# Two transformer blocks on one core: the four FFN up products in Strassen's form

## The chip, the cores and the metric

The kernel runs on 1 core of a Trainium2 chip. The metric is the time of one execution on the device in microseconds (us): 2631.76 us, the median of 3 runs (2631.64 to 2631.97). The core's engines are TensorE (PE; its weight loads are PEld), VectorE (DVE), ScalarE (ACT), GpSimd (POOL) and SyncE (SP), which issues most DMAs.

## What is computed

512 tokens of 1024 channels pass four layers, each a mixer and an FFN with norms and a residual. The mixers (forgetting attention, a gated recurrence, stick-breaking attention with a pool, gated linear attention) are the same in both kernels. Layers 0 and 1 have the SwiGLU FFN, layers 2 and 3 the convolutional one; 2816 hidden channels, gate and up side by side in one weight matrix of 1024 x 5632.

```python
def swiglu_ffn(h, w_in, w_out):
    gate, up = jnp.split(jnp.einsum('bsd,df->bsf', h, w_in), 2, axis=-1)
    return jnp.einsum('bsf,fd->bsd', jax.nn.silu(gate) * up, w_out)

def conv_ffn(h, w_up, conv_w, conv_b, w_down):
    s = h.shape[1]
    u = h @ w_up
    up = jnp.pad(u, ((0, 0), (CONV_WIDTH - 1, 0), (0, 0)))
    conv = conv_b
    for j in range(CONV_WIDTH):
        conv = conv + conv_w[j] * up[:, j:j + s]
    a, g = jnp.split(conv, 2, axis=-1)
    return (jax.nn.silu(a) * g) @ w_down
```

## The kernel before

Activations lie with channels on partitions, 512 tokens in the columns. Every operand of a large product is held as two parts, hi + lo == x: ScalarE casts x to hi, VectorE subtracts to get lo (`split`, L122 to L130). A product is three passes, hi x hi, hi x lo and lo x hi (`mm3`, L242 to L249), so each line L244, L246, L248 has a third of the matmuls.

Weights stream in chunks of 128x1024 fp32, in the order of the `specs` list (`plan_up`, `plan_out` and others): a DMA on SP's queue into one of three raw buffers, a cast (L158) and a subtraction (L159; on GpSimd for chunks marked `early`) into a slot. The slots are W0 to W2, and R or X tiles while they are free. A slot is free again when its matmuls are done (`release`).

An up stage: `up_first` runs six column tiles of 128 for one half of the tokens (256 columns a matmul), while `norm_chain` makes the norm of the other half; its `spread` (L318) puts a value for each token on all partitions. Then come the other half and the remaining column tiles at 512 columns a matmul, two gate tiles and two up tiles in turn. `swiglu_evac` or `conv_evac` takes each finished pair from PSUM (tiles `g`, `a`), computes silu and the product (for the convolution L634 to L636 on ScalarE and VectorE, the last multiply L644 on GpSimd) and splits the result into `hid` (L126, L127). The down product follows.

TensorE issues in the order of the program (`in_order`); small matmuls of a chain are put between the products by a count of columns (`spawn`, `tick`, `due`). The order on the other engines comes from a scheduler at build time. Each engine works through its list in that order.

## Time and profile before

| what | value |
|---|---|
| median of the runs | 2631.76 us |
| profiled execution, span from first to last instruction | 2630.8 us |
| TensorE busy | 2567.0 us, 98%, 13789 matmuls |
| VectorE busy | 1256.5 us, 48% |
| ScalarE busy | 944.0 us, 36% |
| GpSimd busy | 369.0 us, 14% |
| mean granted TensorE clock | 0.989 |
| DMA | 216.91 MB, mean 82 GB/s |

The span and the median differ by 1.0 us, so durations of the profile can be set against the runs. Busy time of TensorE counts overlapping matmuls once; one matmul of 512 columns is shown as 0.39 us long, though the next starts 0.23 us after it. What a stage costs is therefore read from starts, not from durations. Idle time of the other engines costs nothing as long as TensorE doesn't wait for them.

### The profile page before, as it was taken

The page shows a single profiled execution, that of the slowest core. Times are in us where ns is not written, and L with a number is a line of the kernel's source. Part 1 is how long each engine was busy: PE and PEld are TensorE (multiplying, and loading weights), DVE is VectorE, ACT ScalarE, POOL GpSimd, SP SyncE. Part 2 cuts the span into 40 slices and gives each one's busy share as a digit, 9 for nine tenths or more (in the row PEclk, how much of TensorE's full clock was granted, in tenths as well). Part 3 has the DMA queues.
Part 4 walks back from the last instruction along what each step waited for, and adds up shares of the span by engine and source line. Part 5 has one row for each costly group of instructions (what it writes and reads, how often), then busy time and mean ns, then how long its engine had stood idle before and what let it go on. Part 6 is the DMA issues. An engine that isn't in the chain of part 4 may idle for free.

```text
span 2630.8 us, 34163 instructions
## 1 busy us (share of the span) xinstructions
PE 2567.0 (98%) x13789; PEld 2136.0 (81%) x13789; DVE 1256.5 (48%) x2025; ACT 944.0 (36%) x1604; POOL 369.0 (14%) x362
## 2 busy tenths in 40 slices
PE   8999899999899998999999999999999999999999
PEld 6677888888899988988888768888888668888888
DVE  5666543342455564433324675455523344555531
ACT  4445432232222234322323463344422434344421
POOL 0000310000421113000003323111102001211100
PEclk9999999999899999999999999999999999999999
DMA  4223113232212122123322122122332213233331
GB/s 132 72 71 100 58 57 96 91 122 93 81 46 65 52 97 64 56 90 96 120 96 77 57 73 65 57 93 92 120 96 66 65 56 105 65 96 96 96 124 45
DMA packets 224602, 216.91 MB, mean 82 GB/s; under 512 B 9213, under 2 KB 214619, under 8 KB 224443
## 3 DMA queue, kind: packets, MB, share of 16 engines
q1 hardware_dynamic: 222907, 210.15, 25.6%
q0 software_dynamic: 1456, 4.53, 0.6%
q8 instruction: 109, 1.79, 0.3%
q14 instruction: 50, 0.41, 0.1%
q10 hardware_dynamic: 80, 0.03, 0.0%
HBM read 212.55 MB, written 2.13 MB: 82 GB/s over the span
## 4 chain that ended last, share of the span: by engine, by line
PE 92%; DVE 5%; issue 1%; ACT 1%; POOL 0%; DMA 0%; DVEq 0%; ACTq 0%; POOLq 0%
PE g L246 26%; PE g L248 26%; PE g L244 26%; PE a L244 2%; PE a L246 1%; PE a L248 1%; DVE ar L159 1%; PE a L1082 1%; PE m L1082 1%; PE a L1124 1%; PE m L1523 1%; PE m L244 1%; DVE acc L299 1%; DVE h L337 1%; DVE sums L342 0%
## 5 line engine op out<-in xcount | busy, mean ns | idle before, releaser
L159 DVE TENSOR_TENSOR ar<-raw,ar 128x1024 fp32r<-128x1024 f32 (+1 forms) x308 | 381.4, 1239 | 523.1 <-ACT ar L158 522.3
L248 PE MATMUL g<-X,ar 128*128 128x512 f32 (+1 forms) x1568 | 598.9, 383 | 2.6 <-DVE ar L127 2.6
L246 PE MATMUL g<-X,ar 128*128 128x512 f32 (+1 forms) x1568 | 593.7, 379 | 1.5 <-DVE X L127 1.2
L244 PE MATMUL g<-X,ar 128*128 128x512 f32 (+1 forms) x1568 | 589.4, 377 | 5.0 <-ACT ar L126 2.4
L246 PE MATMUL g<-ar 128*128 128x512 f32 (+1 forms) x1608 | 564.6, 351 | 0.2 <-DVE ar L127 0.2
L244 PE MATMUL g<-ar 128*128 128x512 f32 (+1 forms) x1608 | 552.5, 345 | 3.3 <-ACT ar L126 2.6
L248 PE MATMUL g<-ar 128*128 128x512 f32 (+1 forms) x1608 | 552.7, 344 | 0.0
L158 ACT CAST ar<-raw 128x1024 fp32r<-128x1024 f32 (+1 forms) x342 | 354.3, 1038 | 515.0 <-PE g L246 378.9
L246 PEld LDWEIGHTS g<-X,ar 128*128 128x128 f32 x1568 | 297.6, 190 | 66.1 <-DVE X L127 2.3
L244 PEld LDWEIGHTS g<-X,ar 128*128 128x128 f32 x1568 | 296.7, 190 | 65.9 <-ACT ar L126 3.2
L248 PEld LDWEIGHTS g<-X,ar 128*128 128x128 f32 x1568 | 297.5, 190 | 60.3 <-DVE ar L127 3.7
L244 PEld LDWEIGHTS g<-ar 128*128 128x128 f32 x1608 | 307.1, 191 | 41.5 <-issue 6.5
L246 PEld LDWEIGHTS g<-ar 128*128 128x128 f32 x1608 | 308.6, 192 | 31.4 <-issue 3.9
L248 PEld LDWEIGHTS g<-ar 128*128 128x128 f32 x1608 | 308.6, 192 | 27.2 <-issue 1.7
L644 POOL TENSOR_TENSOR a<-a,sg 128x512 f32<-128x512 f32 x44 | 75.1, 1709 | 417.5 <-ACT a L634 323.5
L299 POOL TENSOR_TENSOR acc<-acc,sq 128x512 f32<-128x512 f32 x19 | 27.8, 1464 | 676.1 <-ACT sq L298 623.1
L159 DVE TENSOR_TENSOR X<-raw,X 128x1024 fp32r<-128x1024 f32 (+1 forms) x52 | 57.1, 1099 | 115.5 <-ACT X L158 115.5
L158 ACT CAST X<-raw 128x1024 fp32r<-128x1024 f32 (+1 forms) x60 | 57.7, 962 | 131.2 <-PE g L246 104.3
L159 POOL TENSOR_TENSOR ar<-raw,ar 128x1024 fp32r<-128x1024 f32 x34 | 83.1, 2445 | 126.4 <-ACT ar L158 126.4
L248 PE MATMUL g<-ar,X 128*128 128x512 f32 (+1 forms) x256 | 90.5, 354 | 0.0
L244 PE MATMUL g<-ar,X 128*128 128x512 f32 (+1 forms) x256 | 90.3, 353 | 0.0
L246 PE MATMUL g<-ar,X 128*128 128x512 f32 (+1 forms) x256 | 90.3, 353 | 0.0
(387 smaller groups left out, 3232.7 us busy)
## 6 DMA issues: line engine op xcount, KB each, us to landing
raw<-in_ffn_w_in_dram SPq DMA_DIRECT2D x88, 512.0 KB, 3.4
raw<-in_ffn_w_up_dram SPq DMA_DIRECT2D x88, 512.0 KB, 3.6
raw<-in_ffn_w_out_dram SPq DMA_DIRECT2D x40, 512.0 KB, 3.3
raw<-in_ffn_w_down_dram SPq DMA_DIRECT2D x40, 512.0 KB, 3.4
...
```

Of the source, the lines that this page charges most:

```text
L158: nc.scalar.copy(hi, raw)
L159: (nc.gpsimd if s.early else nc.vector).tensor_sub(lo, raw, hi.bitcast(F32))
L244: mm(ps, ah, bh, start=start, stop=False)
L246: mm(ps, ah, bl, start=False, stop=False)
L248: mm(ps, al, bh, start=False, stop=stop)
L299: eng.tensor_add(acc[:, cols], acc[:, cols], sq[:, :n])
L337: eng.tensor_add(hv, hv, tmp)
L644: nc.gpsimd.tensor_mul(g, g, us[m])
L1082: mm(ps[:M, tt * 64 : (tt + 1) * 64].rearrange("p (b i) -> p b i", i=H), h["k"][:, tt * P : tt * P + M], qv[:, tt * nb // 4 : (tt + 1) * n ...
L1124: nc.tensor.matmul(po[:, c[tt]], lhs, vb[:, s, w], start=s == 0, stop=s == tt)
L1523: mm(po[i * 64 : i * 64 + 64, h * HS : (h + 1) * HS], q[:, 2 * b + h, ck * 64 : (ck + 1) * 64], state[h], start=True, stop=True)
```

## The change

The up product is written as [X11 X12; X21 X22] times [B11 B12; B21 B22]: the rows of blocks are the two halves of the tokens, the inner blocks the two halves of the 1024 channels, the columns 256 gate and 256 up columns. For each of the 11 column blocks seven products of half the size take the place of eight, by Strassen's algorithm in Winograd's variant. Their left operands are a11, a12, s1, s2, s4, s3, a22, made once for an FFN by `combine` in the norm; their right operands are four weight chunks and three differences and a fourth, b12 - b11, b22 - (b12 - b11), b22 - b12, b21 - (...), made in the raw buffers by `pump` before the split (L192), on the engines that `SW` and `CV` name. The results are added while they leave PSUM. The convolution now reads copies in SBUF (`g`, `u`), since its outputs are sums of several products.

`hid` is held in fp32 between up and down; `down` splits it, tile by tile, at its first use. In the up stage there are four slots (W0 to W3) and six raw buffers. The R region changes sides with every FFN; X slots open after down's first column pair. Comment lines are gone throughout.

```diff
-            if slot is None:
+            if slot is None or any(k not in self.raws for k in s.loads):
                 return
             self.free.discard(slot)
+            if s.prep:
+                out, x, y, eng = s.prep
+                getattr(nc, eng).tensor_sub(self.raws[out][1], self.raws[x][1], self.raws[y][1])
             n = s.nk * s.nc
-            reg, o = self.slot_at[slot]
-            hi, lo = reg[:, o : o + n], reg[:, o + 1024 : o + 1024 + n]
-            raw = self.raws.pop(self.n_split)[:, :n]
+            reg = self.slot_at[slot]
+            hi, lo = reg[:, :n], reg[:, 1024 : 1024 + n]
+            raw = self.raws[s.raw][1][:, :n]
             nc.scalar.copy(hi, raw)
             (nc.gpsimd if s.early else nc.vector).tensor_sub(lo, raw, hi.bitcast(F32))
+            for k in s.ends:
+                self.raw_free.append(self.raws.pop(k)[0])
...
+    def combine(self, pool, work, half, gain, R):
+        nc = self.nc
+        lo, hi = slice(0, HS), slice(HS, S)
+        cols = hi if half else lo
+        def norm(c):
+            nc.vector.scalar_tensor_tensor(work[:, c, cols], self.h[:, c, cols], gain[:, c : c + 1], R[:, :HS],
+                                           ALU.mult, ALU.mult)
+        def put(name, k0, src, eng=None, n=2):
+            self.split(src, self.xop(name, 0, k0, n), self.xop(name, 1, k0, n), eng=eng)
+        if not half:
+            for c in range(NC):
+                norm(c)
+                put("a12" if c >= 4 else "a11", c % 4, work[:, c, cols], nc.gpsimd if c in (4, 6) else None, 1)
+            return
+        for c in (0, 4, 1, 5, 2, 6, 3, 7):
+            norm(c)
+        g = (0, 2)
+        a11, a12 = [work[:, k : k + 2, lo] for k in g], [work[:, 4 + k : 6 + k, lo] for k in g]
+        a21, a22 = [work[:, k : k + 2, hi] for k in g], [work[:, 4 + k : 6 + k, hi] for k in g]
+        sums = [pool.tile([P, 2, HS], F32, tag="sums", name="sums", bufs=2) for _ in g]
+        for i in range(2):
+            nc.vector.tensor_add(sums[i], a21[i], a22[i])
+            put("s1", g[i], sums[i])
+        for i in range(2):
+            nc.gpsimd.tensor_sub(a21[i], a11[i], a21[i])
+        for i in range(2):
+            nc.vector.tensor_sub(sums[i], sums[i], a11[i])
+            put("s2", g[i], sums[i])
+        for i in range(2):
+            nc.vector.tensor_sub(a12[i], a12[i], sums[i])
+            put("s4", g[i], a12[i])
+        for i in range(2):
+            put("s3", g[i], a21[i], nc.gpsimd)
+        for i in range(2):
+            put("a22", g[i], a22[i], nc.gpsimd)
...
+    def plan_up(self, tag, w, engines):
+        wv = w.rearrange("(k p) c -> p k c", p=P)
+        src = lambda o, k0, j: wv[:, k0 : k0 + 4, o + j * 256 : o + (j + 1) * 256]
+        early = ["R0", "R1", "R2", "R3", "W0", "W1", "W2"]
+        for j in range(self.EARLY):
+            for k0 in (0, 4):
+                self.want(tag, src(0, k0, j), 4, 256, early, early=j == 0)
+        W = ["W0", "W1", "W2", "W3"]
+        e1, e2, e3, e4 = engines
+        for j in range(NF // 2):
+            add = lambda raw, loads, prep, ends: self.specs.append(
+                Spec(tag, 4, 256, W, False, raw, loads, prep, ends))
+            first = j >= self.EARLY
+            b11 = self.raw(src(0, 0, j), 4, 256, True)
+            if first:
+                b21 = self.raw(src(0, 4, j), 4, 256, True)
+                add(b11, [b11], None, [])
+                add(b21, [b21], None, [])
+            b12 = self.raw(src(FF, 0, j), 4, 256, True)
+            add(b11, [b11, b12], (b11, b12, b11, e1), [])
+            b22 = self.raw(src(FF, 4, j), 4, 256, True)
+            add(b11, [b22], (b11, b22, b11, e2), [])
+            add(b22, [], None, [])
+            add(b12, [], (b12, b22, b12, e3), [b12, b22])
+            if not first:
+                b21 = self.raw(src(0, 4, j), 4, 256, True)
+            add(b11, [b21], (b11, b21, b11, e4), [b11, b21])
+    def product(self, tag, name, ps, start=True):
+        ch = self.get(tag)
+        for m in range(2):
+            w = slice(m * P, (m + 1) * P)
+            for k in range(4):
+                self.mm3(ps[:, m * HS : (m + 1) * HS], ch.hi[:, k, w], ch.lo[:, k, w], self.xop(name, 0, k),
+                         self.xop(name, 1, k), start and m == 0 and k == 0, False, HS, skip=True)
+        self.release(ch)
+    def up_first(self, tag, st):
+        y = [self.bank(), self.bank(), self.abank()]
+        x = [self.bank(), self.bank(), self.abank()]
+        st["xy"] = list(zip(x, y))
+        st["c11"] = []
+        for j in range(self.EARLY):
+            self.product(tag, "a11", x[j])
+            self.product(tag, "a12", y[j])
+            if j < 2:
+                c = self.nrm.tile([P, S], F32, tag="sq", name="c11")
+                self.c11(x[j], y[j], c)
+                st["c11"].append(c)
+    def c11(self, x, y, out):
+        self.nc.scalar.copy(out, x)
+        self.nc.vector.tensor_add(out, y, out)
+    def up(self, tag, st, evac):
+        for j in range(NF // 2):
+            e = evac(j)
+            next(e)
+            if j < self.EARLY:
+                x, y = st["xy"][j]
+                e.send((x, y, st["c11"][j] if j < 2 else None))
+            else:
+                x = self.bank()
+                self.product(tag, "a11", x)
+                y = self.bank()
+                self.product(tag, "a12", y)
+                e.send((x, y, None))
+            z = self.mbank() if j == 1 else self.bank()
+            self.product(tag, "s1", z)
+            e.send(z)
+            self.product(tag, "s2", x, False)
+            e.send(x)
+            self.product(tag, "s4", z, False)
+            e.send(z)
+            self.product(tag, "s3", x, False)
+            e.send(x)
+            v = self.bank()
+            self.product(tag, "a22", v)
+            self.close(e, v)
...
+    def swiglu_evac(self, tp, hid):
+        nc = self.nc
+        def evac(j):
+            new = lambda tag: tp.tile([P, S], F32, tag=tag, name=tag, bufs=2)
+            two = lambda a: a.rearrange("p (m t) -> p m t", m=2)
+            out = [hid[:, 2 * j : 2 * j + 2, h * HS : (h + 1) * HS] for h in range(2)]
+            x, y, g = yield
+            if g is None:
+                g = new("g")
+                self.c11(x, y, g)
+            nc.scalar.activation(g, g, AF.Silu)
+            z = yield
+            p5 = new("p5")
+            nc.scalar.copy(p5, z)
+            x = yield
+            u = new("u")
+            nc.scalar.copy(u, x)
+            z = yield
+            nc.vector.tensor_add(u, z, u)
+            nc.vector.tensor_mul(out[0], two(u), two(g))
+            x = yield
+            u = new("v")
+            nc.scalar.copy(u, x)
+            nc.gpsimd.tensor_add(p5, p5, u)
+            v = yield
+            nc.vector.tensor_add(u, v, u)
+            nc.scalar.activation(u, u, AF.Silu)
+            nc.vector.tensor_mul(out[1], two(p5), two(u))
...
+        def conv(src, ft, u):
             w = lambda j: self.ccol[:, (layer * 3 + j) * 44 + ft : (layer * 3 + j) * 44 + ft + 1]
             bo = 264 + layer * 44 + ft
-            u = tp.tile([P, S], F32, tag=tag, name=tag, bufs=3)
-            nc.scalar.activation(u, ps, AF.Identity, bias=self.ccol[:, bo : bo + 1], scale=w(2))
-            nc.vector.scalar_tensor_tensor(u[:, 1:], ps[:, : S - 1], w(1), u[:, 1:], ALU.mult, ALU.add)
-            nc.vector.scalar_tensor_tensor(u[:, 2:], ps[:, : S - 2], w(0), u[:, 2:], ALU.mult, ALU.add)
-            return u
-        def evac(j, gate, upp, hid):
-            us = [conv(gate[m], 2 * j + m, "sg") for m in range(2)]
+            nc.scalar.activation(u, src, AF.Identity, bias=self.ccol[:, bo : bo + 1], scale=w(2))
+            nc.vector.scalar_tensor_tensor(u[:, 1:], src[:, : S - 1], w(1), u[:, 1:], ALU.mult, ALU.add)
+            nc.vector.scalar_tensor_tensor(u[:, 2:], src[:, : S - 2], w(0), u[:, 2:], ALU.mult, ALU.add)
...
+        def evac(j):
+            two = lambda a: a.rearrange("p (m t) -> p m t", m=2)
+            g = tp.tile([P, 2, S], F32, tag="g", name="g")
+            a = tp.tile([P, 2, S], F32, tag="u", name="u")
+            x, y, c = yield
+            if c is None:
+                nc.scalar.copy(g[:, :, :HS], two(x))
+                nc.vector.tensor_add(g[:, :, :HS], two(y), g[:, :, :HS])
+            else:
+                nc.gpsimd.tensor_copy(g[:, :, :HS], two(c))
+            z = yield
+            p5 = tp.tile([P, S], F32, tag="p5", name="p5")
+            nc.scalar.copy(p5, z)
+            x = yield
+            nc.scalar.copy(a[:, :, :HS], two(x))
+            z = yield
+            nc.vector.tensor_add(a[:, :, :HS], two(z), a[:, :, :HS])
+            x = yield
+            u3 = tp.tile([P, S], F32, tag="u3", name="u3")
+            nc.scalar.copy(u3, x)
+            nc.gpsimd.tensor_add(a[:, :, HS:], two(p5), two(u3))
+            v = yield
+            nc.vector.tensor_add(g[:, :, HS:], two(v), two(u3))
             for m in range(2):
-                nc.scalar.activation(us[m], us[m], AF.Silu)
-                g = conv(upp[m], NF + 2 * j + m, "a")
-                nc.gpsimd.tensor_mul(g, g, us[m])
-                v = g.rearrange("p (h t) -> p h t", h=2)
-                self.split(v, hid(2 * j + m, 0, "F"), hid(2 * j + m, 1, "F"))
+                t = 2 * j + m
+                s = tp.tile([P, S], F32, tag="s", name="s", bufs=2)
+                conv(g[:, m], t, s)
+                nc.scalar.activation(s, s, AF.Silu)
+                conv(a[:, m], NF + t, hid[:, t])
+                nc.gpsimd.tensor_mul(hid[:, t], hid[:, t], s)
...
+    def ffn_up(self, tag, st, evac):
+        side, other = self.r_side, self.other_side()
+        self.free -= set(RS)
+        self.close_r()
+        hp, close_hid = self.open_pool("hid", side)
+        hid = hp.tile([P, NF, S], F32, tag="hid", name="hid")
+        ep, close_ext = self.open_pool("ext", side)
+        self.slot_at["W3"] = ep.tile([P, 2048], F32R, tag="W3", name="W3")
+        self.more_raws(ep, 3)
+        self.vacate("W3")
+        tp, close_tmp = self.open_pool("upt", other)
+        self.up(tag, st, evac(tp, hid))
+        self.less_raws()
+        self.occupy("W3")
+        close_tmp()
+        self.close_xc()
+        close_ext()
+        self.open_r(other)
+        lp, close_tail = self.open_pool("tail", other)
+        self.tail = lp.tile([P, 6144], F32R, tag="tail", name="tail")
+        return hid, close_hid, close_tail
+    def down(self, tag, hid):
+        done = set()
+        def act(k, part, sel):
+            if k not in done:
+                done.add(k)
+                self.split(hid[:, k].rearrange("p (h t) -> p h t", h=2), self.hid(k, 0, "F"), self.hid(k, 1, "F"))
+            return self.hid(k, part, sel)
+        return self.out_gemm(tag, act, list(range(NF)), 1)
...
+    SW = ["vector", "gpsimd", "vector", "gpsimd"]
+    CV = ["gpsimd"] * 4
```

**Order, VectorE, third convolution block or later, before and then now.** Rows are line, operation, output<-inputs; W and ar are weight slots, raw the raw buffers, g PSUM before and SBUF now.

```order
L159 TENSOR_TENSOR ar<-raw,ar 128x1024
L635 SCALAR_TENSOR_TENSOR sg<-g,ccol,sg 128x511
L636 SCALAR_TENSOR_TENSOR sg<-g,ccol,sg 128x510
L159 TENSOR_TENSOR ar<-raw,ar 128x1024
L635 SCALAR_TENSOR_TENSOR a<-g,ccol,a 128x511
L636 SCALAR_TENSOR_TENSOR a<-g,ccol,a 128x510
L159 TENSOR_TENSOR ar<-raw,ar 128x1024
L635 SCALAR_TENSOR_TENSOR a<-g,ccol,a 128x511
L636 SCALAR_TENSOR_TENSOR a<-g,ccol,a 128x510
```

```order
L824 TENSOR_TENSOR g<-g,u_16004 128x2x256
L799 SCALAR_TENSOR_TENSOR hid<-u,ccol,hid 128x511 x2
L800 SCALAR_TENSOR_TENSOR hid<-u,ccol,hid 128x510
L799 SCALAR_TENSOR_TENSOR s<-g,ccol,s 128x511
L800 SCALAR_TENSOR_TENSOR hid<-u,ccol,hid 128x510
L799 SCALAR_TENSOR_TENSOR s<-g,ccol,s 128x511
L800 SCALAR_TENSOR_TENSOR s<-g,ccol,s 128x510
L198 TENSOR_TENSOR W_88<-raw_14865,W_88 128x1024
L198 TENSOR_TENSOR W_14862<-raw_93,W_14862 128x1024
L800 SCALAR_TENSOR_TENSOR s<-g,ccol,s 128x510
L198 TENSOR_TENSOR W_89<-raw_14863,W_89 128x1024
L809 TENSOR_TENSOR g<-g 128x2x256
```

Before, two convolution ops stand between weight splits; now an add that reads the block's last product, then seven of the eight ops, then the next splits.

**Order, GpSimd, all of layer 2's up stage before, and one block of it now.**

```order
L159 TENSOR_TENSOR ar<-raw,ar 128x1024
L311 TENSOR_TENSOR r<-v,mhalf 128x2
L127 TENSOR_TENSOR X<-tmp,X 128x256 x2
L644 TENSOR_TENSOR a<-a,sg 128x512 x22
L299 TENSOR_TENSOR acc<-acc,sq 128x512 x3
L159 TENSOR_TENSOR X<-raw,X 128x1024
```

```order
L822 TENSOR_TENSOR u<-p_15921,u_16004 128x2x256
L192 TENSOR_TENSOR raw_93<-raw_14865,raw_93 128x1024
L831 TENSOR_TENSOR hid<-hid,s 128x512
L192 TENSOR_TENSOR raw_93<-raw_91,raw_93 128x1024
L831 TENSOR_TENSOR hid<-hid,s 128x512
L192 TENSOR_TENSOR raw_14864<-raw_14863,raw_14864 128x1024
L192 TENSOR_TENSOR raw_14863<-raw_14865,raw_14863 128x1024
```

22 multiplies in a stage were all that GpSimd had; now each block has an add, four weight differences (L192) and two multiplies.

**Order, VectorE, from layer 2's up into its down product, before and then now.** R tiles take hid's parts; u_17120 is a buffer's number.

```order
L635 SCALAR_TENSOR_TENSOR a<-g,ccol,a 128x511
L159 TENSOR_TENSOR X<-raw,X 128x512
L127 TENSOR_TENSOR ar<-a,ar 128x2x256
L636 SCALAR_TENSOR_TENSOR a<-g,ccol,a 128x510
L159 TENSOR_TENSOR X<-raw,X 128x1024
L159 TENSOR_TENSOR ar<-raw,ar 128x1024
L127 TENSOR_TENSOR ar<-a,ar 128x2x256
```

```order
L824 TENSOR_TENSOR g<-g,u_17120 128x2x256
L198 TENSOR_TENSOR W_90<-raw_91,W_90 128x1024
L799 SCALAR_TENSOR_TENSOR hid<-u,ccol,hid 128x511 x2
L800 SCALAR_TENSOR_TENSOR hid<-u,ccol,hid 128x510
L799 SCALAR_TENSOR_TENSOR s<-g,ccol,s 128x511
L800 SCALAR_TENSOR_TENSOR hid<-u,ccol,hid 128x510
L799 SCALAR_TENSOR_TENSOR s<-g,ccol,s 128x511
L800 SCALAR_TENSOR_TENSOR s<-g,ccol,s 128x510 x2
L147 TENSOR_TENSOR R_17177<-hid,R_17177 128x2x256 x2
L147 TENSOR_TENSOR R_17178<-hid,R_17178 128x2x256 x2
```

Before, the last two tiles of hid are split here, the other 20 earlier; now the first split of hid stands behind the last block's convolution.

## Rows read from the trace of the kernel before

**Rows 1.** The page: chain of waits, share of the span by engine.

```profile
PE 92%; DVE 5%; issue 1%; ACT 1%; POOL 0%; DMA 0%; DVEq 0%; ACTq 0%; POOLq 0%
```

**Rows 2.** Windows: us; PE, PEld, DVE, ACT, POOL busy; clock; DMA; GB/s.

```profile
326.00:578.00 252.00, 250.75 (x1219) 208.09 (x1219) 94.83 (x122) 75.03 (x107) 7.25 (x8) 1.00 0.27 86
...
1633.00:1889.00 256.00, 251.90 (x1214) 209.87 (x1213) 142.09 (x170) 104.13 (x141) 39.60 (x26) 0.99 0.28 87
...
320.00:326.00 6.00, 6.00 (x30) 6.00 (x31) 1.42 (x5) 0.41 (x1) 3.05 (x2) 0.52 0.42 125
```

**Rows 3.** Timeline, TensorE in an up stage: start, us, line, shape.

```profile
420.05 0.39 PE L246 MATMUL g<-X,ar 128*128 128x512 f32 x1
...
425.65 0.39 PE L246 MATMUL g<-X,ar 128*128 128x512 f32 x1
```

**Rows 4.** Timeline, TensorE around the norm before up0; idle before in brackets.

```profile
306.05 0.28 PE L244 MATMUL g<-ar 128*128 128x256 f32 x1
...
313.85 0.28 PE L248 MATMUL g<-ar 128*128 128x256 f32 x1
319.59 0.98 PE L307 MATMUL m<-invn,acc 128*128 128x1 f32 x4 [5.46 <-DVE acc L343]
...
321.22 0.41 PE L244 MATMUL g<-ar 128*128 128x256 f32 x1
...
323.35 0.41 PE L246 MATMUL g<-ar 128*128 128x256 f32 x1
```

**Rows 5.** Source line 159: count, ns min/median/max, first and last start.

```profile
L159 DVE TENSOR_TENSOR ar<-raw,ar x308: 278/1225/2584, 12.5 to 2587.7; 128x1024 fp32r<-128x1024 f32 x150, 128x512 fp32r<-128x512 f32 x3, 128x128 fp32r<-128x128 f32 x1
...
L159 POOL TENSOR_TENSOR ar<-raw,ar x34: 2345/2397/2847, 288.0 to 2247.0; 128x1024 fp32r<-128x1024 f32 x34
```

**Rows 6.** Source lines 127 and 644, the same columns.

```profile
L127 DVE TENSOR_TENSOR ar<-a,ar x68: 678/687/1625, 261.3 to 2511.7; 128x512 fp32r<-128x512 f32 x64, 64x512 fp32r<-64x512 f32 x4
...
L644 POOL TENSOR_TENSOR a<-a,sg x44: 1287/1710/2152, 1673.1 to 2507.5; 128x512 f32<-128x512 f32 x44
```

**Rows 7.** Groups by form, VectorE and ScalarE: count | busy us, mean ns | idle.

```profile
L352 DVE SCALAR_TENSOR_TENSOR tmp<-h,gcol,m 128x256 f32<-128x256 f32 x112 | 49.7, 475 | 38.9 <-PE m L318 37.8 <-POOL ar L127 0.6
...
L635 DVE SCALAR_TENSOR_TENSOR a<-g,ccol,a 128x511 f32<-128x511 f32 x44 | 32.7, 747 | 73.9 <-ACT a L634 73.9
...
L621 DVE TENSOR_TENSOR a<-g,sg 128x512 f32<-128x512 f32 x44 | 30.2, 691 | 56.3 <-PE g L248 56.1
...
L158 ACT CAST ar<-raw 128x1024 fp32r<-128x1024 f32 x336 | 351.2, 1047 | 507.9 <-PE g L246 372.2 <-issue 86.0 <-PE g L248 21.3
```

**Rows 8.** Timeline, VectorE and GpSimd in a convolution up stage.

```profile
1688.91 1.22 DVE L159 TENSOR_TENSOR ar<-raw,ar 128x1024 fp32r<-128x1024 f32 x1
1690.04 0.75 DVE L635 SCALAR_TENSOR_TENSOR a<-g,ccol,a 128x511 f32<-128x511 f32 x1
...
1691.97 1.62 DVE L127 TENSOR_TENSOR tail<-a,tail 128x512 fp32r<-128x512 f32 x1 [0.40 <-ACT tail L126]
...
1689.13 2.15 POOL L644 TENSOR_TENSOR a<-a,sg 128x512 f32<-128x512 f32 x1 [13.54 <-ACT a L634]
1691.74 1.30 POOL L644 TENSOR_TENSOR a<-a,sg 128x512 f32<-128x512 f32 x1 [0.46 <-DVE a L636]
```

**Rows 9.** Timeline, VectorE and GpSimd in the even mixer; source line 1304.

```profile
1577.79 0.68 DVE L1277 SCALAR_TENSOR_TENSOR B<-B 128x505 f32<-128x505 f32 x1
1578.39 0.96 DVE L1274 TENSOR_TENSOR B<-B 128x7 f32<-128x7 f32 x1
...
1577.99 1.34 POOL L1304 TENSOR_TENSOR w<-w,r 128x384 f32<-128x384 f32 x1 [0.88 <-DVE B L1273]
...
L1304 POOL TENSOR_TENSOR w<-w,r x8: 1007/1014/1746, 1502.1 to 1578.0; 128x384 f32<-128x384 f32 x8
```

**Rows 10.** Timeline, TensorE: second half's spread in two up stages.

```profile
346.15 0.60 PE L318 MATMUL m<-ident,r 128*128 128x128 f32 x4
...
1645.78 1.04 PE L318 MATMUL m<-ident,r 128*128 128x128 f32 x4
```

More of the change, by code (lines that the diff above doesn't have):

```diff
@@ L320, in spread, with norm_chain @@
         return R
-    def norm_chain(self, acc, half, gain, dst, k0, pool=None, y=None, acc_y=None):
+    def norm_chain(self, acc, half, gain, pool=None, y=None, acc_y=None, work=None):
         nc = self.nc
@@ L349, in norm_chain @@
         R = self.spread(r)
+        if work is not None:
+            self.combine(pool, work, half, gain, R)
+            return
         for c in range(NC):
@@ L358, in columns @@
+    def columns(self, pool):
         self.gcol = self.base.tile([P, P], F32, tag="gcol", name="gcol")
-        r = [self.base.tile([64, P], F32, tag=f"r{i}", name=f"r{i}") for i in range(2)]
+        r = [pool.tile([64, P], F32, tag=f"r{i}", name=f"r{i}") for i in range(2)]
         self.nc.scalar.dma_start(r[0], self.t["norm_gains"].rearrange("l n (c p) -> (l n c) p", p=P))
@@ L613, in swiglu_evac @@
[L613 to L623 removed]
+    EARLY = 3
@@ L1566, in sandwich_ffn @@
[L1566 to L1589 removed]
+    net.open_xc()
@@ new lines, in sandwich_out @@
+    yp, close_y = net.open_pool("y", net.other_side())
+    y = yp.tile([P, NC, S], F32, tag="y", name="y")
+    acc, acc2 = net.new_acc(), net.new_acc()
+    chain = lambda half: net.norm_chain(acc2, half, net.gain(layer, 2), yp, y, acc, work=y)
+    g.send(net.y_sink(y, acc, net.gain(layer, 1)))
+    with net.in_order():
+        net.spawn(chain(0))
+        for _ in g:
+            pass
+        net.drain()
+        net.spawn(chain(1))
+        net.up_first(nextup, st)
+        net.drain()
+    close_y()
@@ new lines, in sandwich_ffn, with sink @@
+def sandwich_ffn(net, layer, st, first, gain):
+    side = net.r_side
+    with net.in_order():
+        hid, close_hid, close_tail = net.ffn_up(f"up{layer}", st, net.swiglu_evac)
+        acc, acc2 = net.new_acc(), net.new_acc()
+        late = {}
+        def sink(*args):
+            if not late:
+                close_hid()
+                net.open_e(side)
+                net.pump()
+                late["yp"], late["close"] = net.open_pool("y2", side)
+                late["y"] = late["yp"].tile([P, NC, S], F32, tag="y", name="y")
+                late["sink"] = net.y_sink(late["y"], acc, net.gain(layer, 3))
+            late["sink"](*args)
+        g = net.down(f"down{layer}", hid)
+        chain = lambda half: net.norm_chain(acc2, half, gain, late["yp"], late["y"], acc)
+        next(g)
+        g.send(sink)
+        net.spawn(chain(0))
+        for _ in g:
+            pass
+        net.drain()
+        net.spawn(chain(1))
+        r = first()
+        net.drain()
+    late["close"]()
+    close_tail()
@@ new lines, in conv_ffn, with open_late, sink @@
+    side = net.r_side
+    with net.in_order():
+        hid, close_hid, close_tail = net.ffn_up(f"up{layer + 2}", st, lambda tp, hid: net.conv_evac(tp, hid, layer))
+        late = {}
+        def open_late():
+            close_hid()
+            net.open_e(side)
+            net.pump()
+            late["op"], late["close"] = net.open_pool("outp", side)
+        if out is None:
+            acc = net.new_acc()
+            h_sink = net.h_sink(acc)
+            def sink(*args):
+                if not late:
+                    open_late()
+                h_sink(*args)
+        else:
+            ov = out[0].rearrange("(t p) c -> p t c", p=P)
+            def sink(c, ps, sel):
+                if not late:
+                    open_late()
+                cols = net.cols(sel)
+                nc.vector.tensor_add(net.h[:, c, cols], ps[:, cols], net.h[:, c, cols])
+                tts = range(4) if sel == "F" else (2 * sel, 2 * sel + 1)
+                pt = net.mbank()
+                for tt in tts:
+                    nc.tensor.transpose(pt[:, tt * P : (tt + 1) * P], net.h[:, c, tt * P : (tt + 1) * P], net.ident)
+                ob = late["op"].tile([P, S], F32, tag="ob", name="ob", bufs=3)
+                nc.scalar.copy(ob[:, cols], pt[:, cols])
+                nc.sync.dma_start(ov[:, tts[0] : tts[-1] + 1, c * P : (c + 1) * P],
+                                  ob[:, cols].rearrange("p (t c) -> p t c", t=len(tts)))
+        g = net.down(f"down{layer + 2}", hid)
+        next(g)
+        g.send(sink)
+        if first:
+            net.spawn(net.norm_chain(acc, 0, gain))
+        for _ in g:
+            pass
+        net.drain()
+        if first:
+            net.spawn(net.norm_chain(acc, 1, gain))
+            r = first()
+            net.drain()
@@ L1651, in conv_ffn @@
+    late["close"]()
+    close_tail()
     return r
```

286 lines of the change are left out of this document (99 added, 187 removed).

## Prediction

> **What bounds the kernel now.** I read the chain of waits first: 92% of it is TensorE [rows 1], so nothing shortens the run that doesn't shorten TensorE's row of work, and whatever makes TensorE wait lengthens it. Then the stretches of the four up stages [rows 2]: a SwiGLU stage lasts 252 us with TensorE busy for 250.75 of them at full clock, a convolution stage 256 us with 251.90. VectorE is busy for 95 and 142 us of them, GpSimd for 7 and 40. Then the spacing of the products, because "busy" overlaps from one to the next: 512 columns come every (425.65 - 420.05)/24 = 0.233 us [rows 3], 256 columns every (313.85 - 306.05)/65 = 0.120 us [rows 4]. A block of 256 gate and 256 up columns is 96 products of 512, 22.4 us. Last I read VectorE and GpSimd where they run at the same time [rows 8, 9], since the change gives both much more to do.
>
> **TensorE's own work.** Before, an FFN's up product is 288 products of 256 columns (first three column pairs) and 912 of 512: 34.6 + 212.8 = 247.4 us, which leaves 4.6 and 8.6 us of the stages for norms and waits. After, it is 11 blocks x 7 x 24 = 1848 products of 256: 221.8 us, so 25.6 us less, 102.4 us over four FFNs. That is the gain if TensorE stays the bound. A product of seven takes 24 x 0.120 = 2.88 us, a block 20.2 us; blocks 0 to 2, whose first two are done ahead, 14.4 us.
>
> **What the seven products need.** A block now takes seven splits in place of four (cast on ScalarE, subtraction of the low part on VectorE), and four new differences of 128x1024 weights: two on VectorE and two on GpSimd in the SwiGLU FFNs, all four on GpSimd in the convolution ones. Undisturbed, a 128x1024 subtraction takes 1.225 us on VectorE and 2.40 on GpSimd [rows 5], a 128x512 one 0.687 and 1.287 [rows 6]. ScalarE has seven casts of 1.05 us [rows 7] and about ten ops of half that size, some 13 us: not the bound.
>
> The two engines don't work beside each other, though. At 1689.13 a GpSimd multiply beside VectorE's L159 takes 2.15 us in place of 1.29; at 1691.97 VectorE's L127, 0.69 us alone, takes 1.62 and ends 0.55 us after GpSimd's op does; between them L635, which reads PSUM and SBUF, takes its usual 0.75 beside the same GpSimd op [rows 6 to 8]. So a GpSimd op and a VectorE op that reads two SBUF operands take turns, whole instruction by whole instruction, and their times add. Splits, weight differences and both multiplies into hid read two SBUF operands. The convolution's L799 and L800 in the changed kernel (there a split's subtraction is L198 for weights and L147 for activations) do so too, where L635 and L636 read PSUM. For that form there is one row: the L1277 op at 1577.79 keeps GpSimd's multiply at 1.34 us against 1.014, which in turn holds a VectorE op on seven columns (L1274) for 0.96 us [rows 9]; so I count the form in, and without it is a rival.
>
> The Trainium skill ("SBUF — State Buffer", Who interferes with whom) says that a VectorE instruction with two SBUF inputs contends with a GpSimd instruction that reads SBUF, and that the second fully blocks. By that rule all eight convolution ops of a block belong to the sum; by the FFN rows alone they might not.
>
> **Convolution FFN, a block from the fourth on.** GpSimd: 4 x 2.40 + 3 x 1.287 = 13.5 us. VectorE on two SBUF operands: 7 x 1.225 + 8 x 0.747 [rows 7] = 14.6. In turn: 28.0 us, with three PSUM adds of 0.69 [rows 7] that can lie beside GpSimd. So the block is bound at 28.0 to 30.1 us, 28.5 taken (the order puts the adds next to GpSimd's differences), not at TensorE's 20.2. VectorE's queue shows it too: after L824, which waits for a block's last product, stand seven L799/L800 ops and only then the splits for its fourth product on. Blocks 0 to 2 have two splits fewer: 25.5, taken 26.
>
> **Convolution stage.** The second norm's spread comes 12.6 us after the start [rows 10, 2]. The half's sums and splits then cost 12 VectorE ops of 0.69 and six GpSimd ops of 1.287, 16.0 us in turn (the eight norm ops, 0.475 [rows 7], read PSUM). Then 3 x 26 + 8 x 28.5 = 306; less 8.6 us of the last block's convolution, which come after TensorE's last product, and 3.6 us of block 0 done earlier: 322.4 us. TensorE's 12 us of first products and the stage's old waits lie under that.
>
> **Into the down product.** Before, hid was split while up ran. Now its first split stands on VectorE behind L824, a weight split and all eight convolution ops of the last block: 0.7 + 1.2 + 6.0 + 0.7 = 8.6 us, with GpSimd's two multiplies beside it some 10 us, in which TensorE has nothing. The clock then costs more: after the wait of 5.46 us at 319.59 the products come every (323.35 - 321.22)/10 = 0.213 us [rows 4], at 0.52 of the clock (mostly 1.2 GHz) over 6 us [rows 2], about 3 us lost. So 13 us, and 322.4 + 13 - 256 = +79.4 us for each convolution FFN. The other 21 splits of hid (0.69 each on VectorE, under 1.4 us of TensorE for each row tile) are hidden; if they weren't, at most 10 us more.
>
> **SwiGLU FFN.** In turn: 9 x 1.225 + 2 x 0.69 + 2 x 2.40 + 1.29 = 18.5 us, under TensorE's 20.2. VectorE with its adds has 14.5 us, and 20.6 if every GpSimd op lands on it: 20.6 taken. Blocks 0 to 2: 16.0 in turn against 14.4, 16 taken. The start is worse than now: the spread comes at 346.15, 20.2 us into the stage, with 10 products of the first six left; TensorE reaches the third kind of product at 21.6 us, and what it needs costs 3.8 us of norm ops and the 16.0 in turn, of which it can cover 1.4 and two products, 5.8: about 13 us of waits, and 3 for the clock. At the end an add, a silu, a multiply and the first hid split, 0.7 + 0.6 + 0.7 + 0.7, with steps between some 3.5 us. 21.6 + 13 + 3 + 48 + 165 + 3.5 = 254, +2 us each. If TensorE's 20.2 and 14.4 hold and the start waits only 6 us, 239, or -13; if GpSimd's differences keep the queue late, some +15.
>
> **At nothing:** six more weight loads of 512 KB an FFN (the first blocks' gate columns come twice; a stage's loads share 0.28 of the DMA engines [rows 2], and the stage gets longer); the regions that change sides; the mixers, whose code is the same. Three slots in place of seven in the first column pair of down: a chunk is 5.6 us of TensorE, a split 2.3; without that cover a few us.
>
> **The sum:** the profiled execution spans 2630.8 us, the median is 2631.8, 1 us around it. 2631.8 + 2 x 79.4 + 2 x 2 = 2794.6 us. Bounds: 30.1 and 27.6 a block and SwiGLU at +15, 2857; the floor of the convolution blocks without L799/L800 and the rest as taken is the first rival.
>
> **Rivals.**
> 1. L799/L800 don't take turns with GpSimd. Blocks 22.0 and 19.5; the stage 12.6 + 16 + 58.5 + 176 - 2.6 - 3.6 = 257, with 13 into down +14 each: 2631.8 + 28 + 4 = 2664, 2638 with SwiGLU at -13. Against it: the row at 1577.99, a single one. 15%.
> 2. Faster: the queues keep VectorE and GpSimd out of each other's way, so that TensorE stays the bound in all four stages. It decides where a convolution block comes under the 22.4 us it takes now. 2631.8 - 102.4, with 5 us for each SwiGLU start, 3 for its clock, 3.5 and 13 into down: 2578. For it: the chain is 92% TensorE [rows 1] and 12.5% of these columns go. Against it: 28.0 us of turns in a block can't be reordered away. 8%.
> 3. The clock. Eight us of wait in each convolution block may keep it at 1.2 GHz throughout: 168 x 0.213 = 35.8 us a block, +58 an FFN, 2911. For it: one 5.46 us wait sufficed at 319.59. Against it: in between TensorE has runs of 9 to 12 us. 7%.
> 4. The algebra saves no columns: excluded, the order has 24 products of 256 columns for each of seven products.
>
> **Chances.** Forecast 66%, own range 2735 to 2860; rivals 15, 8 and 7%; 4% for later still. Range for 8 in 10: 2655 to 2862, which takes in most of rival 1. Counting 0.2% as what a measurement of this kernel can tell: faster 10% (rival 2 and the low end of rival 1), the same 3%, slower 87%.
>
> **What would show it.** In the convolution stages: about 28 us from one block's last product to the next's, TensorE waiting 5 us or more a block for VectorE's L198, GpSimd's 128x1024 differences and VectorE's L198 and L799/L800 well over 2.40, 1.225 and 0.75 us, ScalarE under two thirds. L799 at 0.75 beside a GpSimd op would be rival 1. In SwiGLU: blocks at 20.2 to 21 us after a start with waits on s1, s2 and s4. At the start of down a wait of about 10 us for L147 in the convolution FFNs, 3 in the others. The forecast is wrong if a convolution block takes under 24 us.

## The result, and the profile after

The changed kernel takes 2769.14 us (median of 4 runs, 2766.94 to 2770.48) against 2631.86 (2631.64 to 2633.2): a ratio of 1.0517, interval 1.0503 to 1.0532, or 137.3 us more, where 162.8 were forecast. Its profiled execution spans 2768.7 us. Cut at the first product of each up and the first of the down behind it, the two traces compare so:

| stretch | before, us | after, us | difference | forecast |
|---|---|---|---|---|
| SwiGLU up 0 | 251.8 | 250.3 | -1.5 | +2 |
| SwiGLU up 1 | 251.7 | 250.0 | -1.7 | +2 |
| convolution up 2 | 255.5 | 319.1 | +63.6 | +76.4, 3 more in down |
| convolution up 3 | 255.6 | 321.9 | +66.3 | +76.4, 3 more in down |
| all else | 1616.2 | 1627.4 | +11.2 | the 6 above |

The chain of waits, where TensorE had 92% [rows 1], shares of the span by engine:

```profile
PE 72%; DVE 15%; POOL 5%; issue 3%; ACT 3%; DMA 2%; POOLq 0%; SPq 0%; DVEq 0%; ACTq 0%
```

Windows of one SwiGLU and one convolution stage, and below them one convolution block from wait to wait, in three pieces and whole. A product of 256 or 512 columns is one matmul; each of the seven named ones, a11 to a22, is 24 of them. The columns are those of [rows 2]:

```profile
325.37:575.66 250.29, 230.06 (x1864) 227.77 (x1864) 211.56 (x195) 124.70 (x168) 90.92 (x45) 0.96 0.31 97
1632.86:1952.00 319.14, 247.20 (x1858) 242.84 (x1856) 257.26 (x224) 150.64 (x199) 202.69 (x85) 0.87 0.26 81
1842.30:1847.80 5.50, 0.24 (x3) 0.04 (x1) 5.50 (x5) 2.21 (x4) 4.37 (x2) 0.75 0.32 97
1847.80:1851.99 4.19, 4.17 (x20) 4.17 (x21) 4.19 (x3) 1.05 (x1) 3.21 (x2) 0.51 0.21 46
1851.99:1869.60 17.61, 17.61 (x151) 17.61 (x149) 12.63 (x13) 9.89 (x12) 10.25 (x4) 1.00 0.24 79
1842.30:1869.60 27.30, 22.02 (x171) 21.82 (x169) 22.32 (x19) 13.14 (x17) 17.83 (x7) 0.87 0.25 78
```

TensorE, 0.98 busy in the old convolution stage, is busy for 0.77 of the new one. In a block it stands for 5.5 us, then runs 20 products at a granted clock of 0.51 (1.2 GHz), 0.21 us apart, and only then at full speed: 20.0 us of products, 5.4 of wait and 1.9 lost to the clock make the 27.3. Without the convolution the split products work as counted: SwiGLU blocks from the fourth on are 20.0 us apart.

What ends the wait, and what VectorE and GpSimd do ahead of it; from the timeline of a convolution stage (start, us, engine, line; idle before in brackets):

```profile
1869.87 2.34 DVE L198 TENSOR_TENSOR W<-raw,W 128x1024 fp32r<-128x1024 f32 x2
1870.74 2.59 POOL L831 TENSOR_TENSOR hid<-hid,s 128x512 f32<-128x512 f32 x1 [5.32 <-ACT s L829]
1872.14 1.74 DVE L800 SCALAR_TENSOR_TENSOR s<-g,ccol,s 128x510 f32<-128x510 f32 x1
1873.30 2.80 POOL L192 TENSOR_TENSOR raw<-raw,raw 128x1024 f32<-128x1024 f32 x1
1873.80 3.38 DVE L198 TENSOR_TENSOR W<-raw,W 128x1024 fp32r<-128x1024 f32 x1
1874.51 0.57 ACT L808 COPY g<-g 128x512 f32<-128x512 f32 x1
1875.13 0.58 PE L292 MATMUL g<-s,W 128*128 128x256 f32 x1 [5.26 <-ACT g L808]
```

This is the pattern of [rows 8], now with splits, differences, multiplies and taps. L800, 0.74 us alone, waits for GpSimd's L831 to end at 1873.33 and itself ends 0.55 later; L198 waits for L192, which ends at 1876.10, and ends 1.08 later. TensorE's product s2 waits for L808, which copies x into the one gate buffer g; g is free only after the block before's last tap, that L800.

The way into down, VectorE's first split of hid and TensorE behind it:

```profile
1951.98 2.38 DVE L147 TENSOR_TENSOR R<-hid,R 128x512 fp32r<-128x512 f32 x2 [1.26 <-ACT R L146]
1952.00 2.37 PE L292 MATMUL g<-R,W 128*128 128x512 f32 x4 [8.79 <-ACT R L146]
```

### The profile page after: what moved, and what is told of

It reads as the page before. It is cut to its first block, busy times and chain, and to the rows that moved or that the text cites. A ratio compares the mean times of both kernels' runs of the same rounds, so it can differ in the third digit from the quotient of the medians.

```text
span 2768.7 us, 40556 instructions
## 1 busy us (share of the span) xinstructions
PE 2531.9 (91%) x16381; PEld 2247.9 (81%) x16381; DVE 1765.4 (64%) x2373; ACT 1177.6 (43%) x1920; POOL 825.9 (30%) x542
## 4 chain that ended last, share of the span: by engine, by line
PE 72%; DVE 15%; POOL 5%; issue 3%; ACT 3%; DMA 2%; POOLq 0%; SPq 0%; DVEq 0%; ACTq 0%
PE g L292 61%; DVE W L198 4%; PE a L292 3%; POOL raw L192 3%; PE m L292 2%; DVE hid L799 1%; DMA raw<-in_ffn_w_up_dram 1%; DVE s L800 1%; DVE s L799 1%; POOL u L822 1%; DVE y L417 1%; PE a L1302 1%; PE m L1302 1%; DVE hid L800 1%; PE a L1344 1%
## 5 line engine op out<-in xcount | busy, mean ns | idle before, releaser
L198 DVE TENSOR_TENSOR W<-raw,W 128x1024 fp32r<-128x1024 f32 x436 | 673.7, 1552 | 317.2 <-ACT W L197 314.8
L292 PE MATMUL g<-R,W 128*128 128x512 f32 (+2 forms) x3048 | 703.6, 380 | 26.4 <-ACT R L146 25.1
L197 ACT CAST W<-raw 128x1024 fp32r<-128x1024 f32 x455 | 469.3, 1041 | 524.3 <-PE g L292 391.4
L292 PE MATMUL g<-s,W 128*128 128x256 f32 x3840 | 520.4, 299 | 132.5 <-ACT g L808 83.9
L292 PEld LDWEIGHTS g<-s,W 128*128 128x128 f32 x3840 | 506.9, 206 | 141.4 <-ACT g L808 87.2
L292 PEld LDWEIGHTS g<-R,W 128*128 128x128 f32 (+1 forms) x3048 | 515.6, 193 | 122.6 <-ACT R L146 26.6
L192 POOL TENSOR_TENSOR raw<-raw,raw 128x1024 f32<-128x1024 f32 x132 | 346.6, 2626 | 206.1 <-DVE W L198 178.0
L292 PE MATMUL g<-a,W 128*128 128x256 f32 x2784 | 347.3, 285 | 8.4 <-DVE a L147 5.8
L292 PEld LDWEIGHTS g<-a,W 128*128 128x128 f32 x2784 | 339.7, 191 | 10.2 <-DVE a L147 6.6
L292 PE MATMUL g<-W,R 128*128 128x256 f32 (+1 forms) x1224 | 231.6, 335 | 0.0
L292 PEld LDWEIGHTS g<-W,R 128*128 128x128 f32 x1224 | 180.0, 190 | 23.8 <-issue 6.0
L831 POOL TENSOR_TENSOR hid<-hid,s 128x512 f32<-128x512 f32 x44 | 96.6, 2199 | 115.1 <-ACT s L829 107.2
L292 PE MATMUL g<-R,R 128*128 128x256 f32 (+1 forms) x792 | 105.3, 288 | 0.7 <-ACT y L588 0.7
L292 PEld LDWEIGHTS g<-R,R 128*128 128x128 f32 x792 | 99.4, 192 | 2.7 <-ACT y L588 1.1
L198 DVE TENSOR_TENSOR X<-raw,X 128x1024 fp32r<-128x1024 f32 (+1 forms) x39 | 41.2, 1061 | 85.2 <-ACT X L197 85.2
L292 PE MATMUL g<-R,X 128*128 128x256 f32 (+1 forms) x576 | 94.1, 320 | 0.0
L292 PEld LDWEIGHTS g<-R,X 128*128 128x128 f32 x576 | 83.1, 190 | 7.8
L198 POOL TENSOR_TENSOR W<-raw,W 128x1024 fp32r<-128x1024 f32 x19 | 46.4, 2446 | 126.9 <-ACT W L197 117.4
L292 PE MATMUL g<-tail,X 128*128 128x512 f32 (+1 forms) x384 | 81.8, 371 | 0.0
```

Of the source, the lines that this page charges most:

```text
L192: getattr(nc, eng).tensor_sub(self.raws[out][1], self.raws[x][1], self.raws[y][1])
L197: nc.scalar.copy(hi, raw)
L198: (nc.gpsimd if s.early else nc.vector).tensor_sub(lo, raw, hi.bitcast(F32))
L292: self.nc.tensor.matmul(*args, **kw, **(dict(skip_group_check=True) if skip else {}))
L831: nc.gpsimd.tensor_mul(hid[:, t], hid[:, t], s)
```

## Experiments

A block's length is counted from the last product a22 to the next block's, from the fourth block on. Theory A is the prediction's: the sum of what takes turns bounds a block. Theory B is the single buffer g. Theory C, formed after the first four runs, is a chain: last product, add, taps, weight splits in VectorE's order, product s2, with the clock's loss behind the wait. In kernels with new code the lines shift: L294 is L292, L802 and L803 the taps, L819 is L816. Ratios are against the kernel before.

**All differences on VectorE.**

```diff
-    CV = ["gpsimd"] * 4
+    CV = ["vector"] * 4
```

> The four weight differences of each convolution block stand on VectorE, none on GpSimd. In the changed kernel such a block takes 27.3 us, and TensorE waits 5.5 us of it for ScalarE's copy L808. Theory A (turns): the block is as long as the instructions that take turns, VectorE's with two SBUF operands and GpSimd's. The sum falls from 28.0 to 23.4 us (11 x 1.225 + 8 x 0.747 + 3 x 1.29); the block should take 22.8 to 25 us (the PSUM adds no longer lie beside a difference of GpSimd) and the run 2670 to 2720 us. Theory B (one buffer): L808 writes the single gate buffer g, which the block before frees only with its last tap L800; the wait is VectorE's queue from L824 to that tap. VectorE's queue gets 4.9 us more, so the block stays at 26 to 28 us and the run at 2750 to 2785 us.

2755.58 us, 1.0467 (1.0452 to 1.0483): theory A missed, theory B's range held. The turns had 4.6 us less, the block stayed at 27.3, with a wait of 5.8 us for L808 and 13 slow products behind it. TensorE's waits in 1735:1900 (total, times, longest):

```profile
PE g L292 <- ACT g L808: 34.6, 6, 5.8
```

**No differences in the convolution FFNs** (products take weights as loaded).

```diff
-                Spec(tag, 4, 256, W, False, raw, loads, prep, ends))
+                Spec(tag, 4, 256, W, False, raw, loads, prep if prep and prep[3] else None, ends))
...
-    CV = ["gpsimd"] * 4
+    CV = [None] * 4
```

> The weight differences of the convolution FFNs are left out: products s1, s2, s4, s3 use weights as loaded (the output of these FFNs is another); splits, products, adds and taps stay. Theory A: the sum in turn falls to 18.4 us, below TensorE's 20.2; blocks of 20.2 to 20.6 us, no wait for L808, run about 2615 us. Theory B: from the end of a22's product to L808 stand an add (0.7), L798 (0.8), eight taps (5.3), two splits (2.3), L829 (0.6) and L808 (0.6), 10.3 us, less the 8.6 us of a11, a12 and s1: 1.7 us of wait are left, blocks of 21.9 us, run about 2650 us.

2692.81 us, 1.0229 (1.0212 to 1.0246): both missed. Blocks of 24.6 to 26.1 us. The turns bind no longer (they fill 0.68 of the time), but a wait for L808 stays, nearly twice the 1.7 us that theory B leaves, and the clock drops behind it, which neither had counted (13 to 28 products 0.21 us apart; waits as above, then windows of the wait, the 5.3 us behind it and the rest of a block):

```profile
PE g L292 <- ACT g L808: 21.6, 7, 3.1
```

```profile
1838.30:1841.70 3.40, 0.32 (x4) 0.12 (x2) 2.70 (x4) 3.06 (x5) 0.99 (x1) 1.00 0.76 221
1841.70:1847.00 5.30, 5.30 (x32) 5.30 (x33) 0.65 (x1) 0.77 (x1) 1.62 (x2) 0.68 0.48 155
1847.00:1863.20 16.20, 16.20 (x139) 16.20 (x137) 12.36 (x15) 9.22 (x12) 1.78 (x1) 1.00 0.10 34
```

**Two gate buffers.**

```diff
-            g = tp.tile([P, 2, S], F32, tag="g", name="g")
+            g = tp.tile([P, 2, S], F32, tag="g", name="g", bufs=2)
```

> The gate buffer g of the convolution blocks is doubled, so that L808 needn't wait for the taps of the block before; every instruction stays. Theory A: nothing that takes turns goes, so the block stays at 26.5 to 27.3 us with TensorE's wait on another product, run 2755 to 2769 us. Theory B: the wait of 5.5 us goes, blocks of about 21.8 us, run about 2648 us.

2768.14 us, 1.0518 (1.0503 to 1.0534): theory B falls. The wait for L808 is gone, and in the same place stands one for VectorE's split:

```profile
PE g L292 <- DVE W L198: 26.6, 6, 5.2
```

**No taps.**

```diff
-            nc.vector.scalar_tensor_tensor(u[:, 1:], src[:, : S - 1], w(1), u[:, 1:], ALU.mult, ALU.add)
-            nc.vector.scalar_tensor_tensor(u[:, 2:], src[:, : S - 2], w(0), u[:, 2:], ALU.mult, ALU.add)
```

> The two VectorE taps L799 and L800 of the convolution are left out (only the centre tap and bias stay, so the output is another). Theory A: the sum in turn falls by 8 x 0.747 to 22.0 us, blocks of 21.4 to 22 us, the wait before down about 5 us shorter, run about 2630 us. Theory B: the chain to L808 shrinks to 5 us, less than a11, a12 and s1 take, so blocks of 20.2 us and a run of about 2603 us.

2682.44 us, 1.0193 (1.0177 to 1.0208): slower than either. Blocks of 22.1 to 24.4 us, a wait of 2.1 us for L198, and 5.7 and 6.1 us from up's last product to down's first in place of 9.1. Both expectations left out the clock behind a wait; this run doesn't part them.

```profile
PE g L292 <- DVE W L198: 13.4, 7, 2.1
```

**Splits first.** The taps are issued behind the last weight split, and g is doubled.

```diff
+            with self.tc.issue_after(self.last_split.ins):
+                nc.vector.scalar_tensor_tensor(u[:, 1:], src[:, : S - 1], w(1), u[:, 1:], ALU.mult, ALU.add)
...
-            g = tp.tile([P, 2, S], F32, tag="g", name="g")
+            g = tp.tile([P, 2, S], F32, tag="g", name="g", bufs=2)
```

> Two gate buffers, and the taps of a convolution block are issued on VectorE behind the weight split that the block's last product frees; in VectorE's order the splits for s2 and s4 of the next block now stand ahead of the taps. No instruction goes. Theory C (a chain in each block: last product, add, taps, splits, product s2; then TensorE at its lower clock): the wait before s2 falls under 1 us, the clock stays up, blocks of 20.2 to 22 us, run 2637 to 2655 us. Theory A (sum of the turns): 28.0 us of port time less the 0.08 us by which neighbours overlap, 22 times, 26.2 us at least: run 2745 to 2769 us.

2761.99 us, 1.0488 (1.0473 to 1.0504): in theory A's range, and theory C missed. With VectorE's order mended the blocks still take 25.3 to 27.7 us, 26.9 on average; the wait moved to the up half's buffer, which is still single:

```profile
PE g L294 <- ACT u L819: 25.1, 6, 4.5
PE g L294 <- DVE W L198: 2.0, 3, 1.0
```

**Dummy products.**

```diff
+                for _ in range(40):
+                    self.nc.tensor.matmul(d[:, :HS], o[:, :P], o, start=True, stop=True)
```

> 40 products of 256 columns into a bank that nobody reads are added after s1 in each convolution block from the fourth on, 40 x 0.119 = 4.8 us of TensorE, less than the 5.5 us that it waits there. Theory C: the other engines' chain is unchanged, TensorE is not idle and its clock stays up, so that the 18 products at 0.21 us after the wait come at 0.119: 1.7 us a block less, 25.7 us, run about 2742 us, faster with more work. Theory A: the block stays at 27.3 us by the sum of the turns, run 2769 us. If TensorE's own work were the bound, 16 x 4.8 us more, 2846 us.

2748.51 us, 1.0436 (1.0421 to 1.0452): with 640 products more the kernel is 20.6 us faster. Blocks of mostly 26.0 us, 26.2 on average, since two took 28.5 and 28.8; the granted clock of 1735:1890 is 0.99 (first row this run, second the changed kernel):

```profile
1735.00:1890.00 155.00, 149.44 (x1231) 148.22 (x1230) 136.77 (x107) 78.56 (x102) 104.42 (x42) 0.99 0.26 82
```

```profile
1735.00:1890.00 155.00, 125.41 (x950) 124.39 (x950) 126.14 (x100) 71.99 (x93) 103.23 (x41) 0.87 0.26 82
```

So the clock had a part in the block, and 1.1 us of it went with nothing but idle work on TensorE; theory C had forecast 1.7. What ends the 26.2 us that are left isn't parted. Theory A's lower bound is 26.2 (single blocks of 25.3 lie under it), and a wait for the copy into g, here L812, is left too:

```profile
PE g L292 <- ACT g L812: 6.4, 7, 1.9
```

**GpSimd idle in the convolution FFNs** (differences, L822 and L831 on VectorE).

```diff
-            nc.gpsimd.tensor_add(a[:, :, HS:], two(p5), two(u3))
+            nc.vector.tensor_add(a[:, :, HS:], two(p5), two(u3))
...
-                nc.gpsimd.tensor_mul(hid[:, t], hid[:, t], s)
+                nc.vector.tensor_mul(hid[:, t], hid[:, t], s)
...
-    CV = ["gpsimd"] * 4
+    CV = ["vector"] * 4
```

> The four differences, the add L822 and the multiplies L831 of the convolution blocks all stand on VectorE; GpSimd has nothing there, so nothing takes turns. VectorE alone has 11 x 1.225 + 8 x 0.747 + 6 x 0.69 = 23.6 us, 21.6 if each overlaps its neighbour by 0.08. Theory A: blocks of 21.6 to 23.6 us, run 2645 to 2690 us. Theory C: VectorE's queue between the last product and the split for s2 gets no shorter, so blocks stay at 26 to 27.4 us, run 2745 to 2770 us.

2742.15 us, 1.0413 (1.0397 to 1.0428): a little under theory C's range, far over theory A's. With nothing on GpSimd to take turns with, blocks take 25.7 to 27.3 us, 26.8 on average, and wait as before:

```profile
PE g L292 <- ACT g L808: 25.6, 6, 4.3
```

**Both: GpSimd idle and splits first.**

> Both edits: GpSimd has nothing in the convolution blocks, and the splits for s2 and s4 stand ahead of the taps. Left are TensorE's 20.2 us and VectorE's 21.6 to 23.6 us: by theory C blocks of 22 to 24 us and a run of 2650 to 2695 us; by theory A the same as without the new order (2645 to 2690 us), so that this run tells whether the two effects add.

2676.42 us, 1.0161 (1.0144 to 1.0178), blocks of 23.8 us, in both theories' ranges. The two edits don't add, each needs the other: the order alone gave 6.2 us (against two buffers g alone), the idle GpSimd alone 27.0, both 92.7. What is left of waiting is the up half's buffer, up to 2.5 us a block:

```profile
PE g L294 <- ACT u L819: 15.8, 7, 2.5
```

**That buffer doubled too**, with five raw weight tiles in place of six to make room.

```diff
-            a = tp.tile([P, 2, S], F32, tag="u", name="u")
+            a = tp.tile([P, 2, S], F32, tag="u", name="u", bufs=2)
...
-        self.more_raws(ep, 3)
+        self.more_raws(ep, 2)
```

> As the run with GpSimd idle and the splits first, and the up half's buffer doubled too (room for it from one raw weight tile less, five in place of six). There TensorE still waited 2.5 us a block for ScalarE's copy into that single buffer. Theory C: this wait goes, and what is left is VectorE's own 21.6 to 23.6 us: blocks of 21.6 to 22.5 us in place of 23.8, run 2640 to 2655 us. Rival: VectorE's own work already was the bound, or five raw tiles make loads late: blocks 23.5 to 24 us, run 2670 to 2685 us.

2667.23 us, 1.0133 (1.0118 to 1.0148): the blocks came a little under theory C's 21.6 to 22.5, at 21.3 us on average; the total did not come under 2655, since the SwiGLU stages got some 8 and 9 us longer than in the run before this one (blocks of 21.1 us). In the convolution stage VectorE now is the bound, busy for 154.56 of 155 us, and its splits and taps take their undisturbed time (groups by line, mean ns after the busy us; the changed kernel's below):

```profile
1735.00:1890.00 155.00, 147.81 (x1215) 145.44 (x1215) 154.56 (x181) 91.82 (x121) 0.00 (x0) 1.00 0.32 99
```

```profile
L198 DVE TENSOR_TENSOR W<-raw,W 128x1024 fp32r<-128x1024 f32 x51 | 60.9, 1218 | 0.4 <-ACT W L197 0.3
L192 DVE TENSOR_TENSOR raw<-raw,raw 128x1024 f32<-128x1024 f32 x28 | 34.1, 1217 | 0.1
L802 DVE SCALAR_TENSOR_TENSOR hid<-u,ccol,hid 128x511 f32<-128x511 f32 x15 | 11.2, 743 | 0.0
```

```profile
L198 DVE TENSOR_TENSOR W<-raw,W 128x1024 fp32r<-128x1024 f32 x41 | 76.9, 1885 | 17.3 <-ACT W L197 17.3
...
L799 DVE SCALAR_TENSOR_TENSOR hid<-u,ccol,hid 128x511 f32<-128x511 f32 x10 | 13.4, 1383 | 7.1 <-ACT hid L798 7.1
```

**Four early blocks**, on the last kernel and on the changed one.

```diff
-    EARLY = 3
+    EARLY = 4
```

> As the run with both buffers doubled, and the first products of four column blocks in place of three stand ahead of the second norm half, in all four FFNs: 48 products more, 5.7 us of TensorE, to cover the waits of a stage's start (17 us before s1, s2, s4 in the SwiGLU stages). If the start is bound by what VectorE and GpSimd do in turn, each stage gains about 4 us, if by TensorE's lack of work nearly 6: 16 to 23 us less than the run it builds on, 2620 to 2640 us, so at best a little faster than the kernel before. Rival: the waits only move to block 3, the same time as the run it builds on.

2671.71 us, 1.0145 (1.0128 to 1.0162).

> The changed kernel with four early column blocks in place of three and nothing else. By the same working the two SwiGLU stages become 4 to 6 us shorter each; in the convolution stages, where the chain and the turns bound the blocks, 0 to 6. Run 2747 to 2761 us. Rival: no gain, 2769 us.

2787.82 us, 1.0589 (1.0573 to 1.0605). Both missed: each up stage is longer, by 1 to 6 us in the first run and 3 to 7 in the second, and in the second's two SwiGLU stages TensorE's idle time grows from 34 to 37 us. The early block needs its gate weights loaded and split once more; whether that or the banks it holds costs the time stays open.

**Raw tiles by stage.**

```diff
-        self.more_raws(ep, 2)
+        self.more_raws(ep, 2 if tag in ("up2", "up3") else 3)
```

> As the run with both buffers doubled, but five raw weight tiles only in the convolution FFNs, six again in the SwiGLU ones, whose stages with five became 8 and 10 us longer (blocks of 21.1 us in place of 20.0). If the missing raw tile did that, this run takes the 18 us back: about 2650 us, SwiGLU blocks of 20.0 us, the best of the Strassen versions and still 0.7% over the kernel before (12 us a convolution FFN for the way into down, and the waits of each start). Rival: the SwiGLU stages lost by something else (the same 2667 us).

2647.13 us, 1.0055 (1.0041 to 1.0068), near the 2650 expected: SwiGLU blocks at 20.0 us again. It is the fastest form with seven products that was run, 122 us under the changed kernel and still over the one before.

## Why the prediction was right, and where not

**Direction and place: right.** The time is in the two convolution up stages, 130 of the 138 us, and TensorE's columns were saved as counted: blocks of 20.0 us where nothing holds it up, 20.2 forecast.

**Turns: right as a rule.** The taps take turns too, which rival 1 denied: L800 at 1872.14 above, and L799 in the run with the splits first, where the neighbours 0.74 us long show what it takes alone (it is L802 there):

```profile
1838.73 0.74 DVE L802 SCALAR_TENSOR_TENSOR s<-g,ccol,s 128x511 f32<-128x511 f32 x1
1838.89 2.83 POOL L192 TENSOR_TENSOR raw<-raw,raw 128x1024 f32<-128x1024 f32 x1 [2.90 <-DVE W L198]
1839.40 2.87 DVE L802 SCALAR_TENSOR_TENSOR hid<-u,ccol,hid 128x511 f32<-128x511 f32 x1
```

The Trainium skill ("SBUF — State Buffer", Who interferes with whom) states that a VectorE instruction with two SBUF inputs contends with a GpSimd instruction that reads SBUF, and calls the lock between the two exclusive; the rows agree, 2.87 us in place of 0.74, ended 0.55 us after GpSimd's. In 1735:1890 of the changed kernel GpSimd or a VectorE instruction other than the three PSUM adds was at work for 0.93 of the time; for 0.97 in the run with dummies, 0.96 with the splits first. That is 25.4 to 25.7 us a block in all three. One sign was read wrongly: TensorE's wait was forecast for L198, and in the changed kernel it is for L808, behind the tap; it is for L198 only once g is doubled.

**The step that failed: "the block is bound at 28.0 to 30.1 us", by the sum of turns alone.** A block took 27.3 us and looked like that sum; that the number came so near is in part luck. The sum is one limit, and it is too long: neighbours on an engine overlap by 0.08 us (the two L802 above start 0.67 apart and the first takes 0.74), which makes it 26.2, and by the rows the instructions that take turns are at work for 25.4 to 25.7. Beside it lies a second limit that the prediction had only before down: the chain in VectorE's order, last product, add, taps, splits and s2, with the clock behind it. With all differences on VectorE the turn-takers fill 0.80 of the time, with GpSimd idle 0.76, and the blocks still take 27.3 and 26.8 us. Of the runs that keep all of a block's work, only those with both limits gone came clearly away from 27: 23.8 us, and 21.3 with u doubled too. Two things stay open: which of the two ends a block of the changed kernel, and whether the run with the splits first stands at the sum or at u's single buffer, since no run doubled u with GpSimd at work.

**Sizes.** Blocks 1.2 us under the forecast make 8 x 1.2 = 9.6 us a stage, and the first three and the start came 3 us sooner in layer 2 and not at all in layer 3: about the 12.3 and 9.6 us by which TensorE's last product came sooner than at 322.4 us (310.1 and 312.8). The wait before down was 8.8 us (10 forecast), the clock behind it 2.7 (3): 14 products in 6 us at 0.52 of the clock, where at full speed they take 0.233 each.

```profile
1952.00:1958.00 6.00, 6.00 (x14) 4.46 (x15) 6.00 (x9) 6.00 (x12) 1.81 (x2) 0.52 0.01 3
```

**SwiGLU: close.** -1.5 and -1.7 us where +2 stood. Blocks came at 20.0 us, not 20.6, and the second and third at 14.3 to 15.5, not 16; GpSimd's differences found room. The start took 4 us more than forecast (block 0 ends 57.7 us into the first stage, 53.6 by the sum): 3.4 us of waits for VectorE's splits in the first a11, which the sum did not have, stand ahead of 12.5 us (13 forecast) in s1 and s2. Of these for VectorE's split of s:

```profile
PE g L292 <- DVE s L147: 8.6, 3, 5.6
```

**The clock (rival 3): half right.** It fell behind the wait in every convolution block from the fourth on, not for all of it: 1.9 us of 27.3. I had it only before down.

**At nothing: off by some 6 us.** Of the 11.2 us outside the up stages 5.4 are the clock after the two waits before down. The rest is 3.9 us between the second down's first product and the third up's, where a mixer lies, and some 2 elsewhere; their cause wasn't tried.

**Two slips in the working.** The upper bound adds up to 2856 us and rival 1 with SwiGLU at -13 to 2634, where 2857 and 2638 stand; nothing hangs on them.
